# A streaming row maximum that skips NaN: other loads, pieces and reduces in the last sixteen tiles

## The chip, the cores and the metric

The kernel runs on one core of a Trainium2 chip. The metric is the device time of one execution, in microseconds (us); the kernel before was run three times. Five parts of the core matter: the DMA queue that SyncE fills (loads from HBM into on-chip buffers and stores back), and the compute engines ScalarE (ACT in the profile), GpSimd (POOL) and VectorE (DVE). TensorE is not used.

## What is computed

The input is x, 32 x 2048 rows of 2048 float32, in which about one value in ten is NaN. The output is the largest value of each row that is not NaN:

```python
def reference(x: np.ndarray, axis: int) -> np.ndarray:
    return np.nanmax(x, axis=axis).astype(np.float32)
```

The input has 537 MB, the output 0.26 MB, so this is a stream: each byte is read once, cleaned of NaN on the chip and reduced.

## The kernel before

**The work on a piece of x.** x is handled as raw 32-bit words. A NaN shows in the upper 16 bits alone. ScalarE reads the upper halves as int16 and makes a 16-bit "key" from each (line 259 through `act`, called at line 398): for an ordinary value the key is a constant less the half, and for a NaN the slope of the function is such that the key becomes a fixed number. Then the key is written back over the upper halves as "constant less key". An ordinary value comes out as it was, a NaN comes out as a very large negative number. This write-back is done by GpSimd (line 269, `pool`, called at line 419) or, for some pieces, by ScalarE (line 373). After that VectorE takes the float32 maximum over the cleaned words (line 276, `dve`, called at line 444). At the end `find` marks the rows whose maximum is still the replacement value, which must be NaN (lines 282 and 296), and the maxima are stored (line 478).

**Tiles.** x is cut into 74 tiles. All sizes in the table `TILES` are in units of a quarter row, 512 values in each of 128 partitions, which is 256 KB. The first tile has 4 units, each other 28 (7 rows in each partition, 7168 KB). A tile is written as three lists: its loads, its pieces and its reduces. For instance

```python
    + [([28], [7, 9, 12], [16, 12])] * 7
    + [([16, 12], [11, -5, 5, 7], [16, 12])]
```

The first line is seven tiles that each arrive in one load of 28 units, get their keys in pieces of 7, 9 and 12 units, and are reduced 16 and 12 units at a time. In the second there are two loads, and the piece -5, being negative, is written back by ScalarE rather than by GpSimd. Two numbers in brackets, as in (-4, 7), are one key instruction over both, with separate write-backs. A number with a point, as -2.0, is written back by ScalarE too, but only after the key of the next step. A reduce whose end is not the end of a row leaves its result in the last word it has read, and the next reduce takes that word in with the rest of the row.

**Buffers.** There are three buffers for tiles, `xt0` to `xt2` (`BUFS`, line 58), of 7 rows each. Tile n uses buffer (n - 1) mod 3, and its loads wait for the last reduce of tile n - 3. There are three key buffers, `kt0` to `kt2`, of 12 units each (`KEYS`, `NKEYS`). Pieces fill a key buffer as long as they fit; a piece that does not fit goes on to the next and waits until all that was in that one has been written back. When that piece is the last of its tile it also waits for the key buffer after it (line 397).

**Order.** Each engine runs its instructions in the order in which the loops at lines 320 to 456 emit them: tile by tile; in a tile the key of a step, then the ScalarE write-backs that were held, then the write-backs of the step, then each reduce whose units have been emitted. SyncE issues the loads in the order of the table. A class `Order` (line 114) gives every instruction the semaphore waits that it needs and leaves out those that another wait implies. A reduce that needs both a GpSimd and a ScalarE write-back waits for both; for certain pairs `joints` (line 82) finds that one GpSimd and one ScalarE write-back are needed by one reduce alone, and both then count on one semaphore, so the reduce has a single wait. The tiles in `APART` (line 56), 70 to 73, have no such pairs. Loads use 14 semaphores in turn (`LANES`), and a load waits until the load 14 before it has landed.

Of the kernel before, what the change touches and what calls it, by code (L numbers as in the profile page):

```python
# [10 lines left out]
Q = D // 4  # L11
# [19 lines left out]
    + [([28], [6, 10, 12], [16, 12])] * 3  # L31
    + [([28], [7, 9, 12], [12, 16])] * 2
    + [([28], [7, 10, 11], [12, 16])]
    + [([28], [6, 10, 12], [16, 12])] * 3
# [13 lines left out]
)  # L48

GROUPS = [TILES[i : i + 15] for i in range(0, 60, 15)] + [TILES[60:73], TILES[73:]]  # L50
# [2 lines left out]
FLAGGED = (3, 5)  # L53
LATE = 4

APART = (70, 71, 72, 73)
WIDE = 7
BUFS = 3

KEYS = 3 * D  # L60
NKEYS = 3
# [7 lines left out]
TOP = 0x7F7F  # L69
# [9 lines left out]
    return sum(sum(map(abs, p)) if isinstance(p, tuple) else abs(p) for p in pieces)  # L79


def joints(pieces, reds):

    flat = []
    at = 0  # L90
    for step, parts in enumerate(pieces):
        for c in parts if isinstance(parts, tuple) else (parts,):

            flat.append((at, at + abs(c), c < 0, step + isinstance(c, float)))
            at += abs(c)
    needs = []
    done = 0
    for n in reds:
        over = [i for i, (a, b, _, _) in enumerate(flat) if a < done + n and b > done]
        done += n  # L100
        pools = [i for i in over if not flat[i][2]]
        backs = [i for i in over if flat[i][2]]
        if pools and backs and flat[pools[-1]][3] > flat[backs[-1]][3]:
            backs = []
        needs.append(pools[-1:] + backs[-1:])
    pairs = {}
    for need in needs:
        if len(need) == 2 and all(sum(i in n for n in needs) == 1 for i in need):
            for i in need:
                pairs[i] = tuple(need)  # L110
    return pairs
# [61 lines left out]
def kernel(  # L173
# [18 lines left out]
    i16, u16 = mybir.dt.int16, mybir.dt.uint16  # L192
    ALU = mybir.AluOpType
# [19 lines left out]
    warm = lead[:, LEAD // 4 - 1 :]  # L213
    xts = [sbuf(f"xt{i}", WIDE * D, i32) for i in range(BUFS)]
    kts = [sbuf(f"kt{i}", KEYS, u16) for i in range(NKEYS)]
# [49 lines left out]
    def pool(deps, pair=None, **kw):  # L265
        return order.add(
            "pool",
            nc.gpsimd,
            lambda: nc.gpsimd.tensor_scalar(**kw),  # L269
            deps,  # L270
            lane=pair,
            joint=pair is not None,
        )
# [30 lines left out]

    free = [[] for _ in range(BUFS)]
    kfree = [[] for _ in range(NKEYS)]
# [6 lines left out]
    key = 0  # L313
    used = KEYS
    number = 0
# [4 lines left out]
    for gi, (s, g) in enumerate(zip(rows, GROUPS)):  # L320
# [6 lines left out]
        for loads, pieces, reds in g:  # L327
            assert sum(loads) == total(pieces) == sum(reds)
            xt, before = xts[number % BUFS], free[number % BUFS]
            number += 1  # L330
            landed = []
            at = 0
            for c in loads:
                c *= Q
                if ahead:
                    e = ahead.pop(0)
                else:
                    e = load(xt[:, at : at + c], xg[:, base + at : base + at + c], before)
# [4 lines left out]
            at = done = 0  # L343
            reds = [n * Q for n in reds]
            part = []
            held = []
            pairs = {}
            if number not in APART:
                pairs = joints(pieces, [n // Q for n in reds])
            flat = sum((p if isinstance(p, tuple) else (p,) for p in pieces), ())  # L350
            half = {}
            piece = 0

            def cleaned(a, b, k, i, e):

                nonlocal clock
                clock += 1
                both = [(a, b, k, flat[i] < 0, clock)]
                if i in pairs:
                    if pairs[i] not in half:  # L360
                        half[pairs[i]] = both
                        return
                    both += half.pop(pairs[i])
                for a, b, k, back, when in both:
                    kfree[k].append((back, when, e))
                    clean.append((a, b, e))

            def name(i):
                return f"pair{number}_{pairs[i][0]}" if i in pairs else None
# [15 lines left out]
            for parts in pieces:  # L385
                parts = parts if isinstance(parts, tuple) else (parts,)
                c = int(sum(map(abs, parts))) * Q
                here = [l for a, b, l in landed if a < at + c and b > at]
                kold = []
                if used + c > KEYS:  # L390
                    key = (key + 1) % NKEYS
                    used = 0
                    kold, kfree[key] = last(kfree[key]), []
                    assert all(k != key for q in half.values() for _, _, k, _, _ in q)
                    if at + c == sum(loads) * Q:

                        kold = kold + last(kfree[(key + 1) % NKEYS])
                e_key = act(
                    here + kold,
                    out=kts[key][:, used : used + c],  # L400
                    in_=xt[:, at : at + c].bitcast(i16)[:, 1::2],
                    func=ACT.Prelu,
                    bias=EDGE,
                    scale=-1.0,
                    alpha=float(TOP - LOW) / (EDGE - NAN),
                )
                release()
                for c in parts:
                    back, wait, c = c < 0, isinstance(c, float), int(abs(c)) * Q
                    kp = kts[key][:, used : used + c]  # L410
                    used += c
                    to = xt[:, at : at + c].bitcast(i16)[:, 1::2]
                    at += c
                    if back:
                        held.append((at - c, at, key, kp, e_key, piece))
                        if not wait or at == sum(loads) * Q:
                            release()
                    else:
                        e = pool(
                            [e_key],  # L420
                            name(piece),
                            out=to,
                            in0=kp,
                            scalar1=-1.0,
                            scalar2=float(TOP),
                            op0=ALU.mult,
                            op1=ALU.add,
                        )
                        cleaned(at - c, at, key, piece, e)
                    piece += 1  # L430
                    open_ = [h[0] for h in held] + [p[0] for q in half.values() for p in q]
                    while reds and done + reds[0] <= min([at] + open_):
                        n = reds.pop(0)


                        lo = done - 1 if done % D else done
                        done += n
                        row = (base + lo) // D
                        if done % D:
                            m, to = 1, xt[:, done - 1 : done].bitcast(f32)  # L440
                        else:
                            m = max(n // D, 1)
                            to = acc[:, row : row + m]
                        e = dve(
                            [e for a, b, e in clean if b > lo and a < done] + part,
                            nc.vector.tensor_reduce,
                            out=to,
                            in_=xt[:, lo:done]
                            .bitcast(f32)
                            .rearrange("p (c d) -> p c d", c=m),  # L450
                            axis=mybir.AxisListType.X,
                            op=ALU.max,
                        )
                        part = [e] if done % D else []
                        after.append(e)
# [7 lines left out]
        lo, flagged = flagged, first + s  # L463
        if gi == LATE:
            late_acc = maxima(lo, flagged)
        else:
            e = find(
                "dve", nc.vector, after, maxima(lo, flagged), nones[:, lo:flagged], ALU.bitwise_or
            )
            ready += [e] * (gi + 1 - len(ready))  # L470
        if gi == len(GROUPS) - 1:
            e = find("pool", nc.gpsimd, late_after, late_acc, late, ALU.add)
            ready[LATE] = e
    for (og, bits), e in zip(stores, ready):
# [6 lines left out]
            step=16,  # L481
# [38 lines left out]
```

## Time and profile before

| What | Value |
| --- | --- |
| median of 3 runs | 1251.41 us (1251.34 to 1251.47) |
| the profiled execution, its own time | 1251.55 us |
| its span, from the first to the last instruction | 1250.2 us |
| VectorE busy | 1110.8 us, 89%, 181 instructions |
| ScalarE busy | 965.6 us, 77%, 273 instructions |
| GpSimd busy | 1168.5 us, 93%, 242 instructions |
| bytes read and written in HBM | 536.87 MB, 0.26 MB, mean 430 GB/s |

The span is what the profile shows; the profiled execution took 1.3 us more than its span. In the profile a group of instructions is named by line, engine, operation and what it writes and reads, as `L269 POOL TENSOR_SCALAR xt<-kt 128x1536`, with the count, the busy time and the mean duration in nanoseconds behind it, and then the idle time of the engine ahead of them with what ended it. The chain of waits lists, in order of time, the start, the length and the engine of each piece of the chain that ended last. The stage table gives, for a stretch of time, its length, the busy time of each engine with the count of instructions, the clock, the share of time in which the DMA engines were busy, and the GB/s that they moved. The trace also has the moment at which each load has landed.

### The profile page before, as it was taken

Reading aid. Unit: us, or ns where it says so; the run is one execution under the profiler, and the core shown is the slowest. Engines: PE = TensorE matmul, PEld = TensorE weight load, DVE = VectorE, ACT = ScalarE, POOL = GpSimd, SP = SyncE. Lnnn points to the kernel's source line nnn. Section 1 sums busy time; section 2 is a strip of 40 time slices with the busy share of each in tenths; the row PEclk is TensorE's granted clock in tenths of the full one; section 3 lists DMA queues with packets and bytes.
Section 4 is the critical chain, followed back from the end, with each engine's and each line's share of the span. In section 5 each row is a group of like instructions: output and inputs, shape, how many; then the busy total and the mean of one; then the engine's idle time right before and its main releaser. Section 6 shows DMA issues by size and latency. Waiting matters only on the chain.

```text
span 1250.2 us, 878 instructions
## 1 busy us (share of the span) xinstructions
DVE 1110.8 (89%) x181; ACT 965.6 (77%) x273; POOL 1168.5 (93%) x242
## 2 busy tenths in 40 slices
DVE  0888989888889888898988888988888999999999
ACT  3777887778777877788777877777767778999998
POOL 2999989998999899998999899999999999989998
DMA  9999999999999999999999999999999999999997
GB/s 415 438 416 437 440 440 431 420 440 438 438 430 426 440 437 437 424 435 440 435 437 420 440 438 437 433 424 440 437 439 424 433 437 434 430 429 432 429 428 308
DMA packets 15991, 537.20 MB, mean 430 GB/s; under 512 B 2544, under 2 KB 2544, under 8 KB 3568
## 3 DMA queue, kind: packets, MB, share of 16 engines
q1 hardware_dynamic: 15984, 537.14, 99.4%
q14 instruction: 7, 0.06, 0.0%
HBM read 536.87 MB, written 0.26 MB: 430 GB/s over the span
## 4 chain that ended last, share of the span: by engine, by line
DMA 41%; DVE 29%; POOL 19%; ACT 9%; issue 1%; SPq 0%
DMA xt<-in_x_dram 41%; DVE acc L276 22%; POOL xt L269 19%; ACT kt L259 8%; DVE lead L276 7%; ACT xt L259 1%; SPq L235 0%; DVE none L282 0%; DVE lead L296 0%; SPq L253 0%; SPq L244 0%
## 5 line engine op out<-in xcount | busy, mean ns | idle before, releaser
L269 POOL TENSOR_SCALAR xt<-kt 128x3584 int16<-128x3584 uint16 (+11 forms) x236 | 1167.4, 4946 | 78.1 <-ACT kt L259 65.0
L259 ACT ACTIVATE kt<-xt 128x3584 uint16<-128x3584 int16 (+9 forms) x247 | 913.4, 3734 | 276.1 <-DMA xt<-in_x_dram 256.2
L276 DVE TENSOR_REDUCE acc<-xt 128x3 f32<-128x6144 f32 (+3 forms) x119 | 896.2, 7571 | 133.4 <-POOL xt L269 126.1
L276 DVE TENSOR_REDUCE lead<-xt 128x1 f32<-128x2048 f32 (+4 forms) x56 | 211.4, 3850 | 1.1 <-POOL xt L269 0.9
L259 ACT ACTIVATE xt<-kt 128x512 int16<-128x512 uint16 (+6 forms) x24 | 52.9, 2203 | 0.7
L259 ACT ACT_TABLE_LOAD x1 | 1.3, 1283 | 3.3 <-PEq L253 3.3
L302 DVE MEMSET lead<- 128x1 f32 x1 | 0.1, 59 | 3.4 <-PEq L253 3.4
L276 DVE TENSOR_REDUCE xt<-xt 128x1 f32<-128x1536 f32 x1 | 1.7, 1743 | 0.0
L282 DVE TENSOR_SCALAR none<-acc 128x414 int32<-128x414 f32 x1 | 0.6, 593 | 0.0
L282 POOL TENSOR_SCALAR lead<-lead 128x91 int32<-128x91 f32 x1 | 0.5, 547 | 0.1
L296 DVE TENSOR_TENSOR acc<-acc,none 128x414 int32<-128x414 int32 x1 | 0.6, 586 | 0.0
L296 POOL TENSOR_TENSOR lead<-lead 128x91 int32<-128x91 int32 x1 | 0.4, 374 | 0.1
L501 POOL MEMSET const-float32-0.0<- 128x1 f32 x1 | 0.1, 98 | 0.2 <-issue 0.2
L259 ACT ACTIVATE lead<-lead 128x1 f32<-128x1 f32 x1 | 0.2, 202 | 0.0
L282 DVE TENSOR_SCALAR none<-lead 128x7 int32<-128x7 f32 x1 | 0.2, 169 | 0.0
L296 DVE TENSOR_TENSOR lead<-lead,none 128x7 int32<-128x7 int32 x1 | 0.2, 162 | 0.0
L501 POOL MEMSET const-bfloat16-1.0<- 128x1 bf16 x1 | 0.1, 102 | 0.0
L501 POOL MEMSET const-uint8-127<- 128x1 uint8 x1 | 0.1, 101 | 0.0
L501 POOL MEMSET const-float32-1.0<- 128x1 f32 x1 | 0.1, 98 | 0.0
## 6 DMA issues: line engine op xcount, KB each, us to landing
xt<-in_x_dram SPq DMA_DIRECT2D x61, 7168.0 KB, 22.6
xt<-in_x_dram SPq DMA_DIRECT2D x2, 5120.0 KB, 17.5
xt<-in_x_dram SPq DMA_DIRECT2D x3, 2816.0 KB, 22.7
xt<-in_x_dram SPq DMA_DIRECT2D x4, 2048.0 KB, 22.3
xt<-in_x_dram SPq DMA_DIRECT2D x5, 1536.0 KB, 29.1
xt<-in_x_dram SPq DMA_DIRECT2D x2, 3584.0 KB, 24.8
xt<-in_x_dram SPq DMA_DIRECT2D x6, 1024.0 KB, 26.8
xt<-in_x_dram SPq DMA_DIRECT2D x3, 1792.0 KB, 30.3
```

Of the source, the lines that this page charges most:

```text
L259: lambda: nc.scalar.activation(**kw),
L269: lambda: nc.gpsimd.tensor_scalar(**kw),
L276: return order.add("dve", nc.vector, lambda: do(**kw), deps)
L282: lambda: engine.tensor_scalar(out=none, in0=acc, scalar1=NONE, scalar2=float(0x00800000), op0=ALU.is_equal, op1=ALU.mult,),
L296: lambda: engine.tensor_tensor(out=bits, in0=bits, in1=none, op=op),
L302: e_warm = order.add("dve", nc.vector, lambda: nc.vector.memset(warm, 1.0), [])
L501: nc = _bacc.Bacc("TRN2", target_bir_lowering=False, num_devices=1)
```

## The change

Tiles 1 to 58 stay as they are. Tiles 59 to 74 get other loads, pieces and reduces: the last tile 15 loads in place of 9, and pieces of 1 to 3 units. A new form, a positive number with a point, is a piece that GpSimd writes back together with the piece before it, in one instruction over both (`with_last`); both must lie in one key buffer. In `(1, 1), 5.0` GpSimd writes back 1 unit, and then 6 at once. `APART` becomes empty, so tiles 70 to 73 may have pairs on one semaphore as well. The last key of tile 65 (`ALONE`) no longer waits for the key buffer after its own.

```diff
-    + [([28], [6, 10, 12], [16, 12])] * 3
-    + [([28], [8, 11, 9], [8, 8, 12])]
-    + [([20, 8], [11, -6, 6, 5], [16, 12])]
-    + [([20, 8], [12, (-4, 7), 5], [8, 8, 12])]
-    + [([17, 11], [12, (-4, 6), 6], [4, 12, 12])]
-    + [([16, 12], [11, -5, 5, 7], [16, 12])]
-    + [([13, 15], [9, -4, 7, 8], [12, 8, 8])]
-    + [([14, 14], [9, -4, 4, 4, 7], [12, 8, 8])]
-    + [([11, 10, 7], [5, 6, (-3, 7), 7], [4, 4, 4, 8, 8])]
-    + [([11, 9, 8], [4, 7, (-2, 7), 6, -2], [4, 4, 4, 8, 8])]
-    + [([8, 7, 6, 7], [3, 5, 7, (3, -3), 3, 4], [8, 4, 8, 8])]
-    + [([6, 5, 6, 5, 6], [5, (5, -1), (-1, 5), 5, 3, 3], [4, 4, 4, 4, 4, 4, 4])]
-    + [([5, 6, 5, 4, 4, 3, 1], [(-2, 3), 3, 3, (4, -1), 4, 4, -2.0, 2], [4, 4, 3, 1, 4, 4, 4, 4])]
-    + [([4, 4, 3, 2, 4, 2, 3, 3, 3], [2, 2, 4, (-2.0, 1), 2, 3, 3, (-1, 2), (1, -1, 1), 2, -1.0], [4, 4, 4, 4, 4, 4, 4])]
+    + [([28], [7, (2, 9), 10], [12, 12, 4])]
+    + [([28], [6, 10, 12], [16, 8, 3, 1])]
+    + [([28], [12, 12, -4], [12, 12, 1, 3])]
+    + [([28], [(1, 1), 5.0, 10, 11], [4, 12, 12])]
+    + [([16, 12], [-4.0, 12, 12], [4, 12, 12])]
+    + [([17, 11], [-4.0, 12, 12], [16, 12])]
+    + [([17, 11], [11, 6, (4, -7)], [8, 8, 12])]
+    + [([16, 12], [7, 9, 12], [4, 12, 12])]
+    + [([16, 12], [8, 8, -4.0, 8], [8, 8, 12])]
+    + [([14, 14], [5, (6, -1, -2), 6, 8], [4, 8, 8, 8])]
+    + [([10, 10, 8], [(-4, 6), 4, 6, 8], [4, 8, 8, 8])]
+    + [([9, 11, 8], [(6, -3), 5, (4, -2), 4, 4], [8, 4, 8, 4, 4])]
+    + [([8, 8, 6, 6], [(-2, 3, 3), 6, -2, 5, (4, -3)], [4, 4, 8, 4, 8])]
+    + [([8, 7, 6, 7], [4, 4, (4, -2), 3, (3, -1), 3, 4], [4, 4, 4, 4, 4, 4, 4])]
+    + [([5, 4, 4, 3, 4, 3, 1, 4], [(3, -1.0, -1.0), 4, 3, 3, -1, 4, -1.0, 3, 4], [4, 4, 4, 4, 4, 4, 4])]
+    + [([3, 2, 3, 3, 2, 1, 3, 1, 2, 1, 2, 2, 1, 1, 1], [3, (-1, -1.0), 3, 3, -1.0, 2, 2, 2, (1.0, -1.0), 1, 2.0, (-1, 1), 2, -1], [4, 4, 4, 4, 4, 4, 4])]
...
-APART = (70, 71, 72, 73)
+APART = ()
...
+ALONE = (65,)
...
+def with_last(c):
+
+    return isinstance(c, float) and c > 0
...
-            flat.append((at, at + abs(c), c < 0, step + isinstance(c, float)))
+            if with_last(c):
+                flat[-1] = (flat[-1][0], at + abs(c), False, step)
+            else:
+                flat.append((at, at + abs(c), c < 0, step + isinstance(c, float)))
...
-                    if at + c == sum(loads) * Q:
+                    if at + c == sum(loads) * Q and number not in ALONE:
...
-                        e = pool(
...
-                        cleaned(at - c, at, key, piece, e)
-                    piece += 1
+                        group.append((at - c, used - c, key))
+                        if not on:
+                            assert all(k == key for _, _, k in group)
+                            lo, klo, _ = group[0]
+                            e = pool(
+                                [e_key],
+                                name(piece),
+                                out=xt[:, lo:at].bitcast(i16)[:, 1::2],
+                                in0=kts[key][:, klo:used],
+                                scalar1=-1.0,
+                                scalar2=float(TOP),
+                                op0=ALU.mult,
+                                op1=ALU.add,
+                            )
+                            group = []
+                            cleaned(lo, at, key, piece, e)
+                    piece += not on
```

More of the change, by code (lines that the diff above doesn't have):

```diff
@@ L349 @@
                 pairs = joints(pieces, [n // Q for n in reds])
-            flat = sum((p if isinstance(p, tuple) else (p,) for p in pieces), ())
+            each = sum((p if isinstance(p, tuple) else (p,) for p in pieces), ())
+            flat = [c for c in each if not with_last(c)]
+            more = [with_last(c) for c in (*each[1:], 0)]
+            group = []
             half = {}
@@ L408 @@
                 for c in parts:
+                    on = more.pop(0)
                     back, wait, c = c < 0, isinstance(c, float), int(abs(c)) * Q
@@ L411 @@
                     used += c
-                    to = xt[:, at : at + c].bitcast(i16)[:, 1::2]
                     at += c
@@ L418 @@
                     else:
-                        e = pool(
[L420 to L428, printed above, removed]
-                        cleaned(at - c, at, key, piece, e)
-                    piece += 1
-                    open_ = [h[0] for h in held] + [p[0] for q in half.values() for p in q]
+                        group.append((at - c, used - c, key))
[12 more added lines that the diff above has]
+                            )
+                            group = []
+                            cleaned(lo, at, key, piece, e)
+                    piece += not on
+                    open_ = [h[0] for h in held + group] + [p[0] for q in half.values() for p in q]
                     while reds and done + reds[0] <= min([at] + open_):
```

## The prediction

> All times are microseconds from the start of the profiled span unless they are called a run's time. A unit is 512 columns of a row in 128 partitions, 256 KB of x; a tile is 28 units. "Key n" is ScalarE's first pass over n units, "back n" a write-back of n units.
>
> **What bounds the kernel now.** I read the DMA queue's row first, then busy time by stage, then the end of the chain of waits, then the rows by form (for durations), then the landing of each load.
>
> ```profile
> q1 hardware_dynamic: 15984, 537.14, 99.4%
> ```
>
> ```profile
> 1000.00:1053.60 53.60, 50.27 (x9) 39.96 (x11) 52.43 (x10) 1.00 1.00 434
> 1053.60:1180.00 126.40, 125.89 (x28) 118.42 (x42) 117.46 (x28) 1.00 1.00 431
> 1180.00:1223.00 43.00, 43.00 (x16) 40.01 (x22) 41.20 (x17) 1.00 1.00 427
> 1223.00:1242.90 19.90, 19.86 (x11) 19.05 (x17) 18.78 (x13) 1.00 0.97 397
> 1242.90:1250.20 7.30, 5.80 (x5) 2.78 (x4) 3.77 (x5) 1.00 0.04 9
> ```
>
> The queue of loads is full for 99.4% of the span. In the stage rows (length, then VectorE, ScalarE, GpSimd busy, clock, DMA share, GB/s) it stays full to 1242.9, where the last load lands; nothing that the engines do can bring that forward. Only the 7.35 behind it are open. In the same rows VectorE is busy 188.75 of the 189.30 between 1053.6 and 1242.9: from tile 62 on it has no gap, so it is a second line to the same end.
>
> ```profile
> 1242.88 1.02 issue
> 1243.90 0.66 DVE lead L276
> 1244.56 1.53 issue
> 1246.09 2.29 DVE lead L276
> 1248.38 0.02 issue
> 1248.40 0.18 DVE none L282
> 1248.60 0.16 DVE lead L296
> ```
>
> The last reduce starts at 1246.09, 2.19 after the one before it (1243.90), which is the pitch of back-to-back reduces of 4 units. Its inputs end at 1245.91 (GpSimd) and 1245.71 (ScalarE). So both lines meet here: to end earlier, VectorE's line and the path from the last landing must both get shorter. Behind the reduce lie find, store and its wait: 1250.24 - 1248.37 = 1.87, unchanged.
>
> ```profile
> L269 POOL TENSOR_SCALAR xt<-kt 128x6144 int16<-128x6144 uint16 x61 | 429.6, 7043 | 5.9 <-ACT kt L259 1.3
> L269 POOL TENSOR_SCALAR xt<-kt 128x1536 int16<-128x1536 uint16 x10 | 19.0, 1903 | 1.0 <-ACT kt L259 0.3
> L269 POOL TENSOR_SCALAR xt<-kt 128x1024 int16<-128x1024 uint16 x6 | 8.0, 1334 | 0.5
> L269 POOL TENSOR_SCALAR xt<-kt 128x512 int16<-128x512 uint16 x3 | 2.3, 763 | 0.2
> L276 DVE TENSOR_REDUCE lead<-xt 128x1 f32<-128x2048 f32 x28 | 61.9, 2276 | 0.0
> L259 ACT ACTIVATE xt<-kt 128x512 int16<-128x512 uint16 x6 | 4.7, 776 | 0.2
> ```
>
> These give the prices: a GpSimd back of 1, 2, 3, 12 units is 0.76, 1.33, 1.90, 7.04, each with 0.08 between two; a key of 1, 2, 3 units has a pitch of 0.64, 0.95, 1.39, a ScalarE back of 1 unit 0.64; reduces of 4, 8, 12 units follow each other at 2.19, 4.33, 6.47.
>
> **Loads.** The tiles from 59 on are cut into 53 loads where there were 47: tile 72 one fewer, 73 one more, 74 six more. What a load adds: tile 63 (2 loads) lands in 1055.43 - 1038.52 = 16.91, tile 74 (9 loads) in 1242.89 - 1225.49 = 17.40; 0.49/7 = 0.07 for each. Six cost 0.42, so the last landing moves to about 1243.3. Bounds: nothing, if the added time is that of the end and not of the loads; 0.15 each (0.9), twice the dearest excess seen. I take 0.42. The queue stays fed: a load's first packet follows its issue by 1.02 (0.94 to 1.96 at the start), and the buffer for tile 74 is freed by tile 71 at 1201.5, more than 20 before it is needed.
>
> **Catch-up, tiles 59 to 63.** I carry each instruction forward by hand: it starts at the later of its engine's last end and its inputs. The state from tile 58: GpSimd free 991.05, VectorE 999.77. Tile 59 lands at 987.84: key 7 ends 991.05, key 11 995.84, key 10 1000.20. GpSimd: back 7 ends 995.32, 2 runs 995.91 to 997.25, 9 to 1002.65, 10 to 1008.63. VectorE waits for the back of 9, so its first 12 run 1002.69 to 1009.24, the next to 1015.71, the last 4 to 1017.91. Before, this tile was free at 1016.16; the load of tile 62 now goes out 1.75 later, at 1017.94. Tile 61's load lands at 1021.63, so 3.69 are left, and 1.02 are needed: hidden. Tile 60: GpSimd 6, 10, 12 ends 1025.44, VectorE's 16, 8, 3, 1 end 1033.74 (before 1033.04). Tile 61: GpSimd 12, 12 ends 1041.20, 0.69 ahead, since ScalarE takes 4 units; VectorE ends 1050.15 (before 1049.95). Tile 62: one back of 1 and one of 6 (pieces 1 and 5 together), 10, 11, ending 1058.73; VectorE ends its 4, 12, 12 at 1065.32 (before 1065.57). From here VectorE has the line without gaps again, **0.25 ahead**. Tile 63 ends 1080.45 (before 1080.73).
>
> **Tiles 64 to 73.** From 64 to 74 there are 50 reduces as before, and the split row of tile 73 (units 3 and 1, 2.38 instead of 2.19) goes, which saves 0.2. What can break the line is a reduce that waits. Carried forward in the same way, each tile's last back ends before VectorE is done with what it has: GpSimd against VectorE's free time is 1087.79/1088.96 (tile 64), 1119.12/1119.17 (66), 1134.14/1134.27 (67), 1151.50/1151.56 (68), 1166.37/1166.71 (69), 1197.06/1197.13 (71). The margins are 0.05 to 0.3: any longer wait goes straight to the end, as GpSimd needs 16.8 of 16.9 for a tile (4.19 + 5.34 + 7.04 and three gaps) unless ScalarE takes units from it. VectorE's lead over before: 0.34 (64), 0.29 (66), 0.44 (68), 0.57 (70), 0.49 (72), 0.64 (73, end at 1232.37).
>
> **Tile 74.** By 0.6 a unit and 0.07 a load its loads land at 1227.4, 1228.6, 1230.5, 1232.4, 1233.6, 1234.3, 1236.2, 1236.9, 1238.1, 1238.8, 1240.1, 1241.3, 1242.0, 1242.7, 1243.3. ScalarE has 14 keys and 6 backs and starts nearly each as its load lands. GpSimd has 9 backs where there were 11: two of them cover two pieces, each of which saves one fixed part (0.76 + 1.33 - 1.90 + 0.08 = 0.27). The end: key 23-25 at 1241.36, ScalarE's back 1242.43, key 25-27 at 1243.07, key 28 at 1244.01, its back 1244.65 to 1245.43. GpSimd: back 20-23 is 1241.48 to 1243.38, 1 to 1244.22, 2 is 1244.30 to 1245.64. VectorE's reduces start at 1238.89, 1241.19, 1243.42, the last at 1245.68: each released by a back of GpSimd, 0.2 of the lead of 0.64 goes. Against 1246.09 that is **0.41 earlier**. The sum: 1250.24 - 0.41 = 1249.83 of span; the profiled run took 1251.55 with 1.31 around its span, so 1251.14, and since that run lies 0.14 above the median of 1251.41, about **1251.0**.
>
> Both ends. With landings free of the 0.42, VectorE alone decides (1232.28 + 6 x 2.19 = 1245.42): -0.67. With the last loads at 0.15 each, the last back and reduce move 0.5 more: +0.1. Where the hand working is wrong by 1 at one of the tight margins, +0.6. Pairs on one semaphore take away a wait instruction ahead of a reduce (0.02 in the trace) and change no order; the dropped wait of tile 65's last key lets it start when its load lands (1090.13 by ScalarE's own order); I cost both at nothing, VectorE's line covers them.
>
> **Rivals.** (1) *The lines meet as before*: the last tile's keys, 20 ScalarE instructions where there were 15, come 0.3 to 1 late, and the lead is lost: 1251.3 to 1252.2. For it: ScalarE was busy 19.05 of 19.90 there. Against: its last work is 1 unit where it was 3. (2) *Slower by a stall at tile 59*: if key 10 there has to wait for the back of 9 (1002.65) and not of 7, GpSimd's back of 10 ends at 1013.1 in place of 1008.6, tile 59 is freed at about 1022, after the last queued load has landed (1021.63), and GpSimd, which has no slack, carries 4 to the end: 1255. It decides from 2.67 of lateness. Against: the code asks for the buffer one further on only, and the before rows show key 12 starting as the first back ends. (3) *Small loads pay a fixed cost each*: the very first load, alone, took 4.92 for 1 MB, against 2.42 in a full queue, 2.5 more; if the six added loads paid that, 1266. Against: the 256 KB load of tile 73 landed 0.65 behind the one before it, in a full queue. (4) *It gains more than 2.5*: that needs the last landing earlier, which fewer bytes alone would do.
>
> On (3): the Trainium skill, DMA: Bandwidth & Descriptors, section Bandwidth, advises transfers of at least 1 MiB for 75% of peak and has 341 GB/s there; by it, as an estimate, the last tile's 7.34 MB would take 21.5 in place of 17.40, 4 more. The trace does not agree: nine loads of 512 to 1024 KB came at 7.34 MB / 17.40 = 422 GB/s.
>
> **How the numbers follow.** Forecast, 1250.4 to 1251.3: 0.58. Lines meet, 1251.3 to 1252.4: 0.31. Stall: 0.07. Fixed cost of loads: 0.02. More than 2.5 gained: 0.02. The range takes the first two, 1250.2 to 1252.4. 0.2% is 2.5, about what a measurement of this kernel can tell from no change; so within it 0.89, slower 0.09, faster 0.02.
>
> **What the profile after would show.** The last load landing near 1243.3; VectorE without gaps from about 1050; tile 59 free near 1017.9 and tile 62's load issued then, its landing still 1038.5; the last reduce 0.4 earlier, released by GpSimd. Wrong, if the DMA share falls below 1.00 in any stage before 1225, or VectorE waits more than 0.5 in all between 1053 and 1230.

## The result, and the profile after

The changed kernel takes 1254.81 us (median of 9 runs, 1254.61 to 1255.26), the kernel before 1251.41 in the same rounds. The ratio is 1.0028, with a 95% interval of 1.0018 to 1.0038: slower by 3.4, where 0.4 faster was forecast and 1252.4 was the end of the range. The profiled execution has a span of 1253.3 (before 1250.2).

On the page, the queue of loads is busy for 99.2% of the span (99.4% before). Busy time by stage comes next (length, VectorE, ScalarE, GpSimd, clock, DMA share, GB/s):

```profile
1000.00:1053.60 53.60, 50.64 (x15) 42.78 (x13) 50.92 (x11) 1.00 0.99 429
1053.60:1180.00 126.40, 122.91 (x26) 115.89 (x38) 117.22 (x26) 1.00 1.00 432
1180.00:1223.00 43.00, 43.00 (x18) 42.40 (x28) 40.09 (x19) 1.00 1.01 427
1223.00:1243.00 20.00, 20.00 (x10) 19.69 (x21) 18.96 (x11) 1.00 0.99 397
1243.00:1253.30 10.30, 8.48 (x6) 1.78 (x3) 2.83 (x4) 1.00 0.03 6
```

The loads are not the cause. The queue is as full as before, and the last load has landed at 1243.14, against 1242.89 before. What has grown is the stretch behind it: 10.2 where it was 7.35. VectorE is busy 8.48 of the last stage, so it is late, and not its inputs. The stage that made it late is the second one: VectorE is busy 122.91 of 126.40, where it was 125.89. The waits of that stage, in its first 46 us, are three:

```profile
POOL xt L281 <- ACT kt L271: 5.4, 1, 5.4
ACT kt L271 <- POOL xt L281: 4.9, 1, 4.9
DVE lead L288 <- POOL xt L281: 3.5, 1, 3.5
```

Each comes once, and together they are one event. The timeline shows it (start, length, engine, operation; in brackets the idle time ahead and what ended it):

```profile
1058.47 21.29 POOL L281 TENSOR_SCALAR xt<-kt 128x6144 int16<-128x6144 uint16 x3
1072.39 2.47 ACT L271 ACTIVATE xt<-kt 128x2048 int16<-128x2048 uint16 x1
1079.80 17.55 ACT L271 ACTIVATE kt<-xt 128x6144 uint16<-128x6144 int16 x4 [4.94 <-POOL xt L281]
1085.20 17.30 POOL L281 TENSOR_SCALAR xt<-kt 128x6144 int16<-128x6144 uint16 x3 [5.44 <-ACT kt L271]
1092.28 10.98 DVE L288 TENSOR_REDUCE lead<-xt 128x3 f32<-128x6144 f32 x2 [3.49 <-POOL xt L281]
```

This is tile 64, with pieces -4.0, 12, 12. ScalarE ends its write-back of 4 at 1074.86 and then stands still: the key of the last 12 units starts at 1079.80, as GpSimd's first back of 12 ends (1079.76). GpSimd has then nothing to write back until that key is done, 5.44, and VectorE, which had eaten most of its stock, waits 3.49. From there to its last reduce VectorE never waits again, and the chain is VectorE alone:

```profile
1098.84 144.79 DVE lead L288 x45
1243.63 0.84 issue
1244.47 6.68 DVE lead L288 x3
```

Its last reduce starts at 1248.86, though its inputs were there at 1244.98 (GpSimd) and 1244.82 (ScalarE). So nothing in the 150 us behind the stall made up for it.

### The profile page after: what moved, and what is told of

Read it like the earlier page. It is cut to its first block, busy times and chain, and to the rows that moved or that the text cites. A ratio compares the mean times of both kernels' runs of the same rounds, so it can differ in the third digit from the quotient of the medians.

```text
span 1253.3 us, 892 instructions
## 1 busy us (share of the span) xinstructions
DVE 1111.0 (89%) x187; ACT 968.2 (77%) x281; POOL 1165.2 (93%) x240
## 3 DMA queue, kind: packets, MB, share of 16 engines
q1 hardware_dynamic: 16848, 537.14, 99.2%
## 4 chain that ended last, share of the span: by engine, by line
DMA 35%; DVE 34%; POOL 19%; ACT 10%; issue 0%; SPq 0%
DMA xt<-in_x_dram 35%; DVE acc L288 22%; POOL xt L281 19%; DVE lead L288 13%; ACT kt L271 9%; ACT xt L271 1%; SPq L247 0%; DVE none L294 0%; DVE lead L308 0%; SPq L265 0%; SPq L256 0%
## 5 line engine op out<-in xcount | busy, mean ns | idle before, releaser
L281 POOL TENSOR_SCALAR xt<-kt 128x6144 int16<-128x6144 uint16 (+10 forms) x234 | 1164.1, 4975 | 80.5 <-ACT kt L271 66.6
L271 ACT ACTIVATE kt<-xt 128x3584 uint16<-128x3584 int16 (+10 forms) x249 | 912.7, 3705 | 272.7 <-DMA xt<-in_x_dram 242.2
L288 DVE TENSOR_REDUCE acc<-xt 128x3 f32<-128x6144 f32 (+4 forms) x121 | 894.8, 7435 | 133.5 <-POOL xt L281 126.2
L271 ACT ACTIVATE xt<-kt 128x512 int16<-128x512 uint16 (+4 forms) x30 | 57.1, 1912 | 0.6
```

The source lines that it names most:

```text
L271: lambda: nc.scalar.activation(**kw),
L288: return order.add("dve", nc.vector, lambda: do(**kw), deps)
```

## Why that key waits

A key that opens a new key buffer and is the last of its tile also waits for the buffer after its own (`kold + last(kfree[...])`). For tile 64 the next buffer is `kt0`, which holds only the 4 units that ScalarE itself writes back. In the forward working I let that wait be one for the write-back of 4. The waits that the program attaches to each instruction say something else:

```
tile 63, last key: kt2<-xt2 128x6144 [waits order_pool, order_load7, ScalarE's own]
tile 64, last key: kt2<-xt0 128x6144 [waits order_pool, order_load9, order_pair64_1]
```

Tile 64's first reduce takes 16 units, so it needs the 4 from ScalarE and the 12 from GpSimd, and these two become a pair. `cleaned` puts the first of a pair aside, and enters both as free under the later event when the second comes. So "kt0 is free" means "the pair is complete", and the ScalarE key waits for a GpSimd write-back that has nothing to do with its buffer. Tile 63 has the same pieces, but its first reduce takes 4 units, needs ScalarE alone, and makes no pair. In its list the wait for the buffer after its own is ScalarE's own. Tile 65 is exempt from the wait (`ALONE`); tile 64, the one that pays, is not.

That is theory A. Theory B: the loss lies in the many small loads and pieces at the end. Others were added as they came up.

## Experiments

**First set: which wait, and where.** Four versions of the changed kernel with one or two constants changed.

```diff
-ALONE = (65,)
+ALONE = (64,)
```

> The exemption from the wait for the next key buffer is moved from tile 65 to tile 64. Theory A (the loss is the wait of tile 64's last key for the pair's shared semaphore, 4.94 us of ScalarE idle, 5.44 of GpSimd, 3.49 of VectorE, that VectorE never gets back): the stall at 1079.8 goes, but tile 65's last key now waits for GpSimd's back of 11 (about 1094.4 in place of 1090.1 by my forward working); its ScalarE back of 7 ends near 1103.5, tile 66's first key starts 4 later, and VectorE waits about 3.5 at tile 66: 1254.0 to 1255.0, with the gap of VectorE now near 1112 to 1116. Theory B (the loss lies in the fifteen small loads and small pieces at the end): no change, 1254.8, and the VectorE gap at 1088.8 stays or matters not.

Measured: 1255.12 (1254.68 to 1255.63), 0.1 over the forecast of theory A. The stall of tile 64 is gone and one at tile 65 and 66 is there, as forecast. The chain of waits of this run has it in order:

```profile
1087.56 6.48 POOL xt L281
1094.04 0.02 issue
1094.06 4.91 ACT kt L271
1098.97 0.02 issue
1098.99 4.20 ACT xt L271
1103.19 3.04 ACT kt L271
```

Tile 65's last key starts at 1094.06, as GpSimd's back of 11 ends (1094.04), and the ScalarE back of 7 and the key of tile 66 follow it late. VectorE's gaps there come to 3.7. The buffer that tile 65's last key waits for holds a plain GpSimd write-back, no pair. Theory B is out already: the loss moves with a wait 150 us ahead of the end.

```diff
-ALONE = (65,)
+ALONE = (64, 65)
```

> Tiles 64 and 65 are both exempt. Theory A: no gap of VectorE over 0.5 after 1060, the last reduce starts near 1245.7, and the time is 1250.6 to 1251.4, at or a little under the kernel before. Theory B: 1254.5 to 1255. Theory C (the exemption only moves the wait to tile 65's first key, which needs the same key buffer and so the same pair): GpSimd's back ends at 1079.8 and that key's load lands at 1082.3, so by the trace it costs nothing; if C held, the loss would be 2 or more still.

Measured: 1251.07 (1250.80 to 1251.59; before in the same rounds 1251.29; ratio 0.9999, 0.9990 to 1.0008). The whole loss is gone. In the timeline of this run tile 64's last key starts 0.1 ahead of the end of the write-back before it, and GpSimd is idle 0.34 instead of 5.44:

```profile
1072.54 2.47 ACT L271 ACTIVATE xt<-kt 128x2048 int16<-128x2048 uint16 x1
1074.88 5.30 ACT L271 ACTIVATE kt<-xt 128x6144 uint16<-128x6144 int16 x1
1080.26 7.05 POOL L281 TENSOR_SCALAR xt<-kt 128x6144 int16<-128x6144 uint16 x1 [0.34 <-ACT kt L271]
```

The end of its chain is one row of VectorE, from 1048.35 on:

```profile
1048.35 195.40 DVE lead L288 x56
1243.75 1.57 issue
1245.32 2.28 DVE lead L288
```

The last reduce starts at 1245.32; the forecast had 1245.68. The changed kernel has it at 1248.86, which is 3.54 later, for a wait of 3.49. Theory C, that the wait only moves to the next key, falls: that key's load lands at 1082.45, after the pair is complete (1079.93).

```diff
-APART = ()
+APART = (64,)
```

> Only the pair of tile 64 is taken away (its reduce waits for two semaphores); the wait for the next key buffer stays, and is for the ScalarE write-back alone. Theory A says it is the pair that turns this wait into one for GpSimd: 1250.6 to 1251.4, as with both tiles exempt; the last key of tile 64 starts at about 1075. If the wait for the buffer itself were the cost, without the pair: 1254.8. Theory B: 1254.8.

Measured: 1251.55 (1251.30 to 1251.95; ratio to before 1.0002, 0.9993 to 1.0010), 0.15 over the forecast. The wait for the next buffer is kept here, and without the pair it costs nothing: the key starts at 1074.95, where the changed kernel had 1079.80.

```profile
1074.95 5.32 ACT L271 ACTIVATE kt<-xt 128x6144 uint16<-128x6144 int16 x1
```

So at tile 64 it takes both, the wait and the pair; either one alone is free there. The wait alone is not free everywhere: in the run with tile 64 exempt it cost 3.7 at tile 65, where the buffer is GpSimd's in any case.

```diff
-ALONE = (65,)
+ALONE = ()
```

> Dose: no tile is exempt, so tile 65's last key waits for the back of 11 as well (1098.8 in place of 1092.5). Theory A: ScalarE's back of 7 ends near 1108, tile 66's first key and GpSimd's backs come 6 later, VectorE waits a second time, 4 to 5 at tile 66: 1258.5 to 1260. Theory B: 1254.8.

Measured: 1259.95 (1259.61 to 1260.24). VectorE has the old gap, and new ones of 4.9 in all at the end of tile 65 and in tile 66, about as forecast:

```profile
1092.50 15.28 DVE L288 TENSOR_REDUCE lead<-xt 128x3 f32<-128x6144 f32 x3 [3.54 <-POOL xt L281]
1108.20 6.55 DVE L288 TENSOR_REDUCE lead<-xt 128x3 f32<-128x6144 f32 x1 [0.41 <-ACT xt L271]
1115.51 2.29 DVE L288 TENSOR_REDUCE lead<-xt 128x1 f32<-128x2048 f32 x1 [0.76 <-POOL xt L281]
1120.91 6.55 DVE L288 TENSOR_REDUCE lead<-xt 128x3 f32<-128x6144 f32 x1 [3.12 <-POOL xt L281]
1128.06 124.15 DVE L288 TENSOR_REDUCE lead<-xt 128x3 f32<-128x6144 f32 x41 [0.60 <-POOL xt L281]
```

**Second set: the same mechanism mended, planted and taken away elsewhere.**

```diff
-    + [([17, 11], [-4.0, 12, 12], [16, 12])]
+    + [([17, 11], [-4.0, 12, 12], [4, 12, 12])]
```

> The changed kernel with one reduce of tile 64 cut in two: [4, 12, 12] in place of [16, 12], as tile 63 has it with the same pieces. The ScalarE write-back of 4 is then alone behind the first reduce, so it forms no pair; the wait for the next key buffer stays. Theory A (a reduce that joins both write-backs makes the buffer's wait one for GpSimd): tile 64's last key starts near 1075, no gap of VectorE, 1250.8 to 1251.6, although a reduce is added. Theory D (the exemption or its lack is what matters, whatever the reduce): 1254.8.

Measured: 1251.48 (1251.23 to 1252.04; ratio to before 1.0002, 0.9993 to 1.0011). One more reduce on the busiest line, and 3.3 faster. VectorE has no wait over 0.15 between 1030 and 1248.

```diff
-ALONE = (65,)
+ALONE = (64, 65)
...
-    + [([16, 12], [-4.0, 12, 12], [4, 12, 12])]
+    + [([16, 12], [-4.0, 12, 12], [16, 12])]
```

> Planted stall: the version with tiles 64 and 65 exempt (1251.07), with one reduce fewer in tile 63: [16, 12] in place of [4, 12, 12]. No instruction is added. Theory A: tile 63's write-back of 4 and its first back of 12 become a pair, the tile's last key waits for the back (1065.6 in place of starting at 1060.2), GpSimd's second back starts 5.4 later, VectorE waits 3.4 to 3.9 before its second reduce of tile 63: 1254.4 to 1255.2. Theory D (fewer reduces can only help, VectorE is the line): 1250.9 to 1251.1.

Measured: 1256.32 (1255.96 to 1256.58). The stall is planted, with one instruction fewer in the kernel, but it costs 5.25 over the version without it, more than I wrote. The timeline tells why:

```profile
1066.14 12.34 ACT L271 ACTIVATE kt<-xt 128x6144 uint16<-128x6144 int16 x3 [5.53 <-POOL xt L281]
1071.55 14.17 POOL L281 TENSOR_SCALAR xt<-kt 128x6144 int16<-128x6144 uint16 x2 [5.44 <-ACT kt L271]
1078.62 6.55 DVE L288 TENSOR_REDUCE lead<-xt 128x3 f32<-128x6144 f32 x1 [3.79 <-POOL xt L281]
1085.75 15.15 DVE L288 TENSOR_REDUCE lead<-xt 128x4 f32<-128x8192 f32 x2 [0.58 <-POOL xt L281]
```

The first gap is the forecast one. But with GpSimd 5.4 late the next tile's tight margin breaks as well (0.58). And 0.55 were lost ahead of it: the reduce of 16, which stands where 4 and 12 stood, needs the back of 12, which ends at 1066.12, while VectorE was free at 1065.60. A further 0.41 at 1052 belongs to this execution: its tile 62 had landed 0.5 later than in the version that it is compared with.

```diff
-APART = (70, 71, 72, 73)
+APART = ()
```

> The kernel before, with pairs allowed in tiles 70 to 73 too. The keys that then wait for a pair (tiles 71, 72 and 74) start 10 us or more after that pair's later write-back has ended in the trace of before, so theory A gives no change, 1251.2 to 1251.5. Theory E (a shared semaphore costs something by itself): 0.5 or more slower.

That is the kernel before. Measured: 1251.35 (1251.10 to 1251.46; before 1251.30). Pairs whose write-backs are long done cost nothing, so theory E falls on this side.

```diff
-ALONE = (65,)
+ALONE = (64, 65)
...
-APART = ()
+APART = tuple(range(75))
```

> The version with tiles 64 and 65 exempt, with no pair in any tile: each reduce that needs both engines waits for two semaphores, a wait instruction of 0.02 more. Theory A: what pairs are worth here is at most some tenths, as VectorE has no gap: 1250.8 to 1251.8. Theory E (pairs matter by themselves): outside of that.

Measured: 1251.57 (1251.42 to 1251.88), against 1251.07 with the pairs. VectorE has no wait over 0.15 in either. What pairs bring lies within the intervals, at most some tenths.

**Third set: the terms of the end.** These are about the 0.4 that had been forecast.

```diff
-ALONE = (65,)
+ALONE = (64, 65)
...
-    + [([3, 2, 3, 3, 2, 1, 3, 1, 2, 1, 2, 2, 1, 1, 1], [3, (-1, -1.0), ...
+    + [([1] * 28, [3, (-1, -1.0), ...
```

> The version with tiles 64 and 65 exempt (1251.07; last landing 1243.38, last back of GpSimd 1245.10, last reduce at 1245.32), with the last tile's 15 loads cut into 28 of 256 KB each, pieces unchanged. If a small load costs 0.07 in a full queue (my term): thirteen more move the last landing by 0.9 to 1244.3, the last back to about 1246.0 and the last reduce to 1246.1, 0.8 later: 1251.7 to 1252.1. If each pays the 2.5 that a load alone pays: 1280 or more.

Measured: 1250.90 (1250.61 to 1251.56; before in these rounds 1251.09; ratio 0.9998, 0.9989 to 1.0008). A miss: 1251.7 to 1252.1 was forecast. The last tile's loads take 1243.41 - 1224.85 = 18.56, where the 15 took 1243.38 - 1225.26 = 18.12: thirteen more for 0.44. But the 15 loads of the other profiled executions took 17.46 to 18.18, so one difference of this size does not give a price. In this execution the loads had also reached the last tile 0.4 earlier, so the last landing is the same, and the last store landed 0.3 sooner after its issue (see below), so the time is no longer either. A fixed cost of 2.5 a load is out in any case.

```diff
-ALONE = (65,)
+ALONE = (64, 65)
...
-    + [([3, 2, 3, 3, 2, 1, 3, 1, 2, 1, 2, 2, 1, 1, 1], ...
+    + [([4, 4, 3, 2, 4, 2, 3, 3, 3], [2, 2, 4, (-2.0, 1), 2, 3, 3, (-1, 2), (1, -1, 1), 2, -1.0], [4, 4, 4, 4, 4, 4, 4])]
```

> The version with tiles 64 and 65 exempt, with the last tile as before (9 loads, the last of 3 units, 11 keys). If the path from the last landing binds: the last back ends at 1245.9 as in the trace of before and the last reduce starts near 1246, 0.6 to 0.7 later: 1251.4 to 1251.8. If VectorE's line alone sets the end: the last reduce at 1245.3 as it is, 1251.0 to 1251.2.

Measured: 1251.50 (1251.31 to 1252.10), in the range of the first case, but not by its way. The profiled execution is the slowest of the ten (1252.10). In it the last reduce starts at 1246.65, 0.33 after GpSimd's last back has ended (1246.32) and right behind the reduce before it. So the path from the last landing does not bind. VectorE had waited 0.54 at 1233.06 and 0.27 at 1235.61 for GpSimd's first backs of the last tile, and from there its six reduces follow without a gap:

```profile
1235.61 13.31 DVE L288 TENSOR_REDUCE lead<-xt 128x1 f32<-128x2048 f32 x6 [0.27 <-POOL xt L281]
```

With the new last tile these waits are not there. It also shortens the path from the last landing to GpSimd's last back (1.72 against 3.43 here), although its loads land later (1243.38 against 1242.89).

The last run is the kernel before with its last tile alone replaced by the new one, and `with_last` in the code:

```diff
-    + [([4, 4, 3, 2, 4, 2, 3, 3, 3], [2, 2, 4, (-2.0, 1), ...
+    + [([3, 2, 3, 3, 2, 1, 3, 1, 2, 1, 2, 2, 1, 1, 1], [3, (-1, -1.0), ...
```

> The kernel before with the new last tile alone (15 loads, small pieces, its pairs). VectorE's line, which is as before up to tile 73, sets the end: the last reduce stays near 1246.1 although its inputs are there near 1245.1 to 1245.6: 1251.2 to 1251.5. If the path from the last landing was the only bound: 0.4 to 0.6 less.

Measured: 1251.37 (1251.15 to 1251.47). The last reduce starts at 1245.71, its inputs end at 1245.41: VectorE's line holds it. That it lies 0.4 ahead of before goes with the loads of this execution, which reached the last tile 0.37 earlier (1225.12 against 1225.49); the kernel before with pairs in all tiles, whose loads were as early (1225.11), has its last reduce at 1245.73 with the old last tile. So the new last tile alone moves nothing.

The versions of the changed kernel in the first two sets together, by the waits of VectorE over 0.15 each after 1050, in the profiled execution:

| Version | VectorE waits | Time |
| --- | --- | --- |
| 64 and 65 exempt | 0 | 1251.07 |
| no pair at 64 | 0 | 1251.55 |
| reduce of 64 cut | 0 | 1251.48 |
| no pairs, 64 and 65 exempt | 0 | 1251.57 |
| the changed kernel | 3.5 | 1254.81 |
| 64 exempt alone | 3.7 | 1255.12 |
| pair planted at 63 | 5.3 | 1256.32 |
| none exempt | 8.4 | 1259.95 |

Against the mean of the first four, 1251.42, the losses are 3.4, 3.7, 4.9 and 8.5: to within 0.4, what VectorE waits after 1050 is what the kernel loses.

## Why the prediction was wrong, point by point

**The step that failed** stands in two sentences of it. One gives tile 64's last back as ended before VectorE is free, "1087.79/1088.96"; the profile has 1092.25 and 1088.79. The other says that pairs on one semaphore "change no order", and puts their cost "at nothing". The waits that a pair adds to the engine that reuses a key buffer were not looked at, only those of the reduce. The list of the program's waits, which needs no run, names the pair on that key. It cost 4.94 of ScalarE, 5.44 of GpSimd and 3.49 of VectorE.

**A second term was wrong, the end behind the last reduce.** It was put at 1.87, "unchanged". From the end of the last reduce to the end of the span it is 2.18 in the changed kernel and 2.16 with 64 and 65 exempt. The last store takes longer from issue to landing, before and after:

```profile
out_dram<-lead SPq DMA_DIRECT2D x1, 3.5 KB, 1.4
out_dram<-lead SPq DMA_DIRECT2D x1, 3.5 KB, 1.7
```

All nine profiled executions with 15 loads in the last tile have 1.56 to 1.72 here; the three with nine loads and the one with 28 have 1.40 to 1.42. Why stays open.

**The price of a stall was right.** "Any longer wait goes straight to the end", and the condition "VectorE waits more than 0.5 in all between 1053 and 1230" both held. I gave a stall 0.07 and a time of 1255, but the one that I described sat at tile 59, which ran as worked out (freed at 1017.54, forecast 1017.91; tile 62's load issued at 1017.57, and nothing starved). That 1255 lies so near to 1254.81 is luck. The other sign of being wrong, a DMA share below 1.00 before 1225, also showed, 0.99 from 1000 to 1053.6; but the kernel before with pairs in all tiles had 0.99 there too, at 1251.35, so it says nothing.

**The rest of the working came out nearly right in the version without the stall.** GpSimd's backs of tiles 64, 66 and 67 end at 1087.31, 1118.96 and 1133.95 (forecast 1087.79, 1119.12, 1134.14), the last landing is at 1243.38 (forecast 1243.3). VectorE's last reduce starts at 1245.32 (forecast 1245.68), and not released by GpSimd, whose last back ends at 1245.10, but on VectorE's own line. It is 0.36 early and the end behind it 0.3 longer than forecast: that 1251.07 meets the forecast of 1251.0 is in part two errors that cancel. The other three versions without the stall have 1251.48 to 1251.57, so a gain of 0.4 is not shown; all four are level with before within what can be measured.

**The cost of a load** was put at 0.07. One pair of executions gives 18.12 - 17.40 = 0.72 for six more loads, 0.12 each, but the spread between executions is as large. The means are 17.31 (three executions with nine loads), 17.86 (nine with 15) and 18.56 (one with 28): by these, as an estimate, 0.09 and 0.05 for each. So 0.07 is neither confirmed nor refuted.

**One row was misread.** VectorE does have a gap before, 0.42 at 1059.02, so it is without gaps from there and not "from tile 62 on". No step rests on it.

**The rivals.** The small-load rival is out: 7.34 MB in 28 loads of 256 KB came at 7.34 MB / 18.56 = 395 GB/s, and not at the 341 that the Trainium skill, DMA: Bandwidth & Descriptors, section Bandwidth, has for 1 MiB in transfers that GpSimd issues; the measurement decides, for loads in a full queue. That both lines must get shorter at once is not shown by the times: the last two runs, each of which shortens only one, end level with before, but so do the versions that shorten both.

## What to carry to other kernels

When two instructions are made to count on one semaphore, as here, everyone who waits for one of them waits for both: look up every waiter, the reuse of buffers too, and not only the consumer for whom they were joined. Where an engine has no gap up to the end, a wait far upstream costs its full length (here 3.49 at 1088.79, and 3.54 at the last reduce); read the waits of the stage in which that engine last had to wait, not the last microseconds. A worked-out order is to be laid beside the list of waits that the program really has before it is believed.

## What was not expected of the hardware

A queue of loads that is kept full hardly minds their size here: 28 loads of 256 KB took 18.56, 2 loads of the same 7168 KB in tile 63 took 16.91, and 15 loads 17.46 to 18.18. Over 26 more loads that is 0.06 each (an estimate from these two times), while the kernel's first load of 1 MB took 4.92 from issue to landing.

The last store, 3.5 KB, landed 1.40 to 1.42 after its issue with nine or 28 loads in the last tile, and 1.56 to 1.72 with 15. No run here shows the cause.
